# RWKV time mixing: unit-by-unit columns in the mixed tiles of four batches, and another order for the last unit

## The chip, the cores and the metric

One core of a Trainium2 chip runs the kernel. The metric is the device time of one execution in microseconds (us), given as the median of several runs. Beside it stands one profiled execution, whose records give every instruction's start and duration.

## What is computed

x has 16 batches of 2048 tokens of 256 values, in f32. Each token is mixed with the token before it in its batch (zero ahead of the first), once with the weights of R and once with those of V. The result is projected, gated and projected once more. The key projection of the full layer does not reach the output, so the kernel leaves it out.

```python
x_prev[:, 1:, :] = x[:, :-1, :]
xv = x * time_mix_v + x_prev * (1 - time_mix_v)
xr = x * time_mix_r + x_prev * (1 - time_mix_r)
v = xv @ value_weight
r = xr @ receptance_weight
out = (sigmoid(r) * v) @ output_weight
```

## The kernel before

**Tiling.** The tokens are cut into 64 units of 512 tokens, four to a batch; unit g is quarter e = g % 4 of batch b = g // 4. The 256 channels lie on the 128 partitions in two halves, counted by `ko`. So a unit of mixed input is 128 partitions x (2 x 512) bf16 elements, in a shape with the channels on the partitions (x transposed). Time mixing is done up to a factor that the weights `w_bf` absorb: mixed = c * x + x_prev, with one constant c per channel (`c_sb`). Because x_prev is x one column earlier, the second term is the same transposed tile `xt` read with an offset of one token.

**Where the transposed tiles come from.** Batches 0 to 9 are transposed by TensorE (L271) and copied out by ScalarE (L288). Batches 10 to 15 are staged in DRAM in bf16 and come back through two DMA transposes on the SP queue (L253), three batches each. In batches 2 to 9 a column index is (j, c) with token = c * 16 + j (in batches 0 and 1 the same within a unit, token = c * 4 + j); in batches 10 to 15 the columns of `xt` are the tokens in their natural order.

**Pairs of units.** From unit 10 on, two units (1024 tokens) share a mix tile, and the product c * x is made for both units at once, in three pieces of 128x1024: `scale` on VectorE (L353) for half ko = 0 of R, `scale_act` on ScalarE (L631) for half ko = 0 of V (from unit 36 on), and `scale_pool` on GpSimd (L363) for half ko = 1 of both. The sum with x_prev is made unit by unit, on VectorE, by `add` (L375). A mix tile thus has a writer that sees a pair and a writer and a reader that see one unit.

**Batches 10 to 13** (`STAGED_PAIRS`, units 40 to 55) need a special order of columns. Their output is stored per pair of units with eight consecutive tokens to a partition row, so token = q * 8 + h * 4 + i, where q is the output partition (0 to 127), h the unit within the pair, and i runs from 0 to 3. A unit h therefore owns four columns of every eight, in `xt` and, in this kernel, also in the mix tile: `unit_cols` (L319) splits the columns as `(q h i)` and takes one h. Reading a unit out of such a tile means rows of four bf16 elements at a distance of eight. For a pair, `unit_cols` gives the columns back as they are. Batches 0 to 9 and batches 14 and 15 have each unit's columns of the mix tile in rows of 128 or more, without that interleaving.

**One unit's work.** `project` (L383) makes R into the PSUM tile `psum_r`, four matmuls with a moving operand of 128x512 from the mix tile; ScalarE takes the sigmoid into `s_sb` (L651). `project` makes V into `psum_v` in the same way; VectorE multiplies both into `z_sb` (L690). `out_matmuls` (L412) makes the output into `psum_o`, eight matmuls with z as the stationary operand and 256 columns of weight; ScalarE copies it to SBUF (L464), and `store` (L433) sends it out, from the SP queue. Each of `psum_r`, `psum_v` and `psum_o` has one buffer of two banks, and the pool `ps_t` has two of one bank.

**Order.** The program is written out by hand in loop order (the framework's own scheduling is off); within an engine the instructions run in that order. From g = 33 on TensorE's order in iteration g is R of unit g, output of unit g - 2, V of unit g. VectorE's is: scale, sums, z of the unit, sums. The last iterations return to the output of unit g - 1, and outputs of units 60 and 61 go in halves through the `ps_t` pool.

**The last unit** (`last_unit`, L481 on; g = 63) cuts everything finer. R and V of unit 63 are projected in halves of 256 tokens; `receptance(h)` makes a half of R and its sigmoid (L497), `value(h, n)` a half of V and its product z (L503), in pieces of n * 128 columns. `out_part(pool, name, z, b, e, jj, n, copy, queue)` makes n of a unit's four output slots of 128 tokens, copies them with the engine named (`by_act` or `by_dve`, L442) and stores them from the queue named. With n = 2 its stationary operands are z columns with a step of two (`(c j)`); with n = 1 they are 128 columns in a row. z of unit 62 is written in two halves of 256 columns. The four PSUM banks of the half projections are taken up front: `psum_r`, `ps_t`, `psum_v`, `ps_t`.

Two lines carry what the change touches: the layout, and the piece that the last unit's outputs are made of.

```python
return cols.rearrange("p k (q h i) -> p k q h i", h=2, i=UJ)[:, :, :, lo // TU % 2]
order = "p k (j c) -> p k j c" if b < STAGED else "p k (c j) -> p k j c"
```

Of the kernel before, what the change touches and what calls it, by code (L numbers as in the profile page):

```python
# [15 lines left out]
def kernel(  # L16
# [25 lines left out]
    nc = tc.nc  # L42
# [5 lines left out]
    UJ = 4  # L48
    TU = UJ * P
# [5 lines left out]
    H = UJ // 2  # L55
# [41 lines left out]
    ps_t_pool = ctx.enter_context(tc.tile_pool(name="ps_t", bufs=2, space=bass.MemoryType.PSUM))  # L97
    ps_v_pool = ctx.enter_context(tc.tile_pool(name="ps_v", bufs=1, space=bass.MemoryType.PSUM))
    ps_r_pool = ctx.enter_context(tc.tile_pool(name="ps_r", bufs=1, space=bass.MemoryType.PSUM))
    ps_o_pool = ctx.enter_context(tc.tile_pool(name="ps_o", bufs=1, space=bass.MemoryType.PSUM))  # L100
# [12 lines left out]
    xt = {}  # L113
# [199 lines left out]
    def slots(piece, off=0):  # L313

        b, _, lo, hi = piece
        j = lo // P + (lo // TU if b < BYUNIT else 0) + off
        return slice(j, j + (hi - lo) // P)

    def unit_cols(cols, lo, hi):  # L319

        if hi - lo > TU:
            return cols
        assert hi - lo == TU
        return cols.rearrange("p k (q h i) -> p k q h i", h=2, i=UJ)[:, :, :, lo // TU % 2]

    def tokens(piece, off, ko=None):

        b, _, lo, hi = piece
        if b in STAGED_PAIRS:
            pair = lo // (2 * TU) * 2 * TU + off  # L330
            cols = unit_cols(xt[b][:, :, pair : pair + 2 * TU], lo, hi)
            return cols if ko is None else cols[:, ko]
        if b < STAGED:
            cols = xt[b][:, slots(piece, off)]
        else:
            cols = xt[b][:, :, off + lo : off + hi].rearrange("p k (j c) -> p j k c", c=P)
        return cols if ko is None else cols[:, :, ko]

    def mixed(piece, ko=None):
        b, m, lo, hi = piece  # L340
        cols = mix[(b * S + lo) // (2 * TU)][:, m]
        if b in STAGED_PAIRS:
            cols = cols.rearrange("p j k c -> p (j k c)").rearrange("p (k t) -> p k t", k=KO)
            cols = unit_cols(cols, lo, hi)
            return cols if ko is None else cols[:, ko]
        j = lo // P % (2 * UJ)
        cols = cols[:, j : j + (hi - lo) // P]
        return cols if ko is None else cols[:, :, ko]

    def scale(piece, kos=(0, 1)):  # L350
        b, m, _, _ = piece
        for ko in kos:
            nc.vector.tensor_scalar(  # L353
                out=mixed(piece, ko),
                in0=tokens(piece, 0, ko),
                scalar1=c_sb[:, m, ko : ko + 1],
                scalar2=None,
                op0=ALU.mult,
            )

    def scale_pool(piece, after):
        b, m, _, _ = piece
        op = nc.gpsimd.tensor_scalar(  # L363
            out=mixed(piece, 1),
            in0=tokens(piece, 0, 1),
            scalar1=c_sb[:, m, 1:2],
            scalar2=1.0,
            op0=ALU.mult,
            op1=ALU.mult,
        )  # L370
        tc.add_manual_dep(op.ins, after.ins.name, SYNC, reason="one at a time")

    def add(piece):
        b = piece[0]
        return nc.vector.tensor_tensor(  # L375
            out=mixed(piece), in0=mixed(piece), in1=tokens(piece, 1), op=ALU.add
        )

    def project(ps, g, m, lo=0, hi=TU):
        b, e = divmod(g, UB)  # L380
        for mo in range(KO):
            for ko in range(KO):
                nc.tensor.matmul(  # L383
                    out=ps[:, mo, :],
                    lhsT=w_bf[:, m, ko, mo * P : (mo + 1) * P],
                    rhs=mixed((b, m, e * TU + lo, e * TU + hi), ko),
                    start=(ko == 0),
                    stop=(ko == KO - 1),
                )
# [15 lines left out]
    def out_matmuls(ps, z, b, jj, n):  # L405

        cols = z[:, :, jj * P : (jj + n) * P]
        order = "p k (j c) -> p k j c" if b < STAGED else "p k (c j) -> p k j c"
        slot = cols.rearrange(order, j=n)
        for j in range(n):  # L410
            for ko in range(KO):
                nc.tensor.matmul(  # L412
                    out=ps[:, j, :],
                    lhsT=slot[:, ko, j],
                    rhs=wo_bf[:, ko, :],
                    start=(ko == 0),
                    stop=(ko == KO - 1),
                )

    def store(queue, b, lo, hi, after=None):  # L420
        src = o_sb[b, lo // (2 * UJ)]
        j = lo % (2 * UJ)
        src = src[:, j : j + hi - lo, :]
        if b < STAGED:
            dst = out[b].rearrange("(p j) d -> p j d", p=P)[:, lo:hi, :]
        elif b in STAGED_PAIRS:
            h = lo // (2 * UJ)
            dst = out[b, h * 2 * TU : (h + 1) * 2 * TU].rearrange("(p j) d -> p j d", p=P)[:, j : j + hi - lo]
        else:
            n = min(hi - lo, UJ)  # L430
            dst = out[b, lo * P : hi * P].rearrange("(e p j) d -> p e j d", p=P, j=n)
            src = src.rearrange("p (e j) d -> p e j d", j=n)
        op = queue.dma_start(out=dst, in_=src)  # L433
        if after is not None:
            tc.add_manual_dep(op.ins, after.ins.name, SYNC, reason="in turn with the last load")

    def out_part(pool, name, z, b, e, jj, n, copy, queue):
        ps = pool.tile([P, n, D], FP32, name=name)
        out_matmuls(ps, z, b, jj, n)
        lo = e * UJ + jj  # L440
        j = lo % (2 * UJ)
        copy(out=o_sb[b, e // 2][:, j : j + n, :], in_=ps)  # L442
        store(queue, b, lo, lo + n)

    def new_o(b, h):

        n = b * UB // 2 + h - SPARE
        spare = n >= 0 and n % (NO + NX) < NX
        pool, name = (xpool, "x_bf") if spare else (opool, "o_sb")
        o_sb[b, h] = pool.tile([P, 2 * UJ, D], FP32, name=name)  # L450
# [30 lines left out]
    def last_unit(g):  # L481


        b, e = divmod(g, UB)
        new_o(b, e // 2)
        s_sb = zpool.tile([P, KO, TU], BF16, name="s_sb")
        z_sb = zpool.tile([P, KO, TU], BF16, name="z_sb")
        cols = [(h * H * P, (h + 1) * H * P) for h in range(2)]
        spare = [(ps_r_pool, "psum_r"), (ps_t_pool, "ps_t"), (ps_v_pool, "psum_v"), (ps_t_pool, "ps_t")]
        banks = [pool.tile([P, KO, H * P], FP32, name=name) for pool, name in spare]  # L490

        by_act, by_dve = nc.scalar.copy, nc.vector.tensor_copy

        def receptance(h):
            lo, hi = cols[h]
            project(banks[h], g, 0, lo, hi)
            nc.scalar.activation(out=s_sb[:, :, lo:hi], in_=banks[h], func=ACT.Sigmoid)  # L497

        def value(h, n):
            lo, hi = cols[h]  # L500
            project(banks[2 + h], g, 1, lo, hi)
            for c in range(lo, hi, n * P):
                nc.vector.tensor_tensor(  # L503
                    out=z_sb[:, :, c : c + n * P],
                    in0=s_sb[:, :, c : c + n * P],
                    in1=banks[2 + h][:, :, c - lo : c - lo + n * P],
                    op=ALU.mult,
                )

        receptance(0)  # L510
        out_part(ps_o_pool, "psum_o", z_prev, b, e - 1, 0, H, by_dve, nc.sync)
        receptance(1)
        value(0, H)
        out_part(ps_r_pool, "psum_r", z_prev, b, e - 1, H, H, by_act, nc.sync)
        value(1, 1)
        out_part(ps_v_pool, "psum_v", z_sb, b, e, 0, 1, by_act, nc.sync)
        out_part(ps_o_pool, "psum_o", z_sb, b, e, 1, 1, by_act, nc.sync)
        out_part(ps_t_pool, "ps_t", z_sb, b, e, 2, 1, by_act, nc.scalar)
        out_part(ps_t_pool, "ps_t", z_sb, b, e, 3, 1, by_dve, nc.sync)

    def tile_for(b):

# [80 lines left out]
    by_act = {g: [] for g in range(-1, NU)}  # L603
# [35 lines left out]
    for g in range(NU - 1):  # L639
# [47 lines left out]
        z_sb = zpool.tile([P, KO, TU], BF16, name="z_sb")  # L687
# [13 lines left out]
        if g in STAGE_AT:  # L701
            b = STAGE_AT[g]
# [7 lines left out]
        if g == 1:  # L710
            advance(4)
        z_prev2, z_prev = z_prev, z_sb
    last_unit(NU - 1)


# [28 lines left out]
```

## Time and profile before

| | |
|---|---|
| median of 3 runs | 200.34 us (200.04 to 200.56) |
| profiled execution | 200.75 us |
| its span, first to last instruction | 198.9 us |
| TensorE clock granted | 0.997 of full |
| busy share | TensorE 97%, VectorE 92%, ScalarE 89%, GpSimd 44% |
| chain that ended last | TensorE 87%, VectorE 5%, DMA 3% |
| bytes moved by DMA | 58.13 MB, mean 292 GB/s |

All times inside the execution are counted from the start of the span. [...] the distance from one group to the next says more than the duration of one. The chain view does that: it lists the pieces on the way to the last instruction, each with the time that it added.

### The profile page before, as it was taken

To read this page: it belongs to the slowest core of one execution; us is meant where nothing else is said; L and a number is where in the kernel's file an instruction comes from. 1 tells how busy PE (TensorE), PEld (TensorE's weight loads), DVE (VectorE), ACT (ScalarE), POOL (GpSimd) and SP (SyncE) were. 2 spreads that over 40 slices of the span, in tenths; PEclk is the share of its full clock that TensorE was granted. 3 is DMA by queue.
4 is the path that set the end of the run, shared out by engine and by line. 5 is a ranking of instruction groups with operands and counts; after the bars stand their busy time and mean duration, and the time that the engine had idled before them with its cause. 6 is when DMAs were issued, how large, how long until landed. Compare 5 with 4: busy or idle time off the path is not lost.

```text
span 198.9 us, 3759 instructions
## 1 busy us (share of the span) xinstructions
PE 193.8 (97%) x1368; PEld 123.5 (62%) x1368; DVE 183.8 (92%) x287; ACT 177.0 (89%) x197; POOL 86.8 (44%) x117
## 2 busy tenths in 40 slices
PE   8999999999999999999999999999999999999992
PEld 4656676666666666666666566656655666666661
DVE  0899999999999999999999999999999999999972
ACT  3699899999999999999999999998888888899972
POOL 2846442443675634624424474444443344444200
PEclk9999999999999999999999999999999999999998
DMA  5999999999999999999999999999999999999585
GB/s 176 236 184 216 221 278 274 270 256 260 247 384 272 292 315 321 290 226 222 234 276 290 416 293 222 208 273 228 290 340 420 415 412 422 415 417 413 244 319 202
DMA packets 36553, 58.13 MB, mean 292 GB/s; under 512 B 26068, under 2 KB 27448, under 8 KB 32312
## 3 DMA queue, kind: packets, MB, share of 16 engines
q1 hardware_dynamic: 32368, 41.34, 59.7%
q0 software_dynamic: 4016, 16.44, 41.2%
q8 instruction: 10, 0.16, 0.3%
q10 hardware_dynamic: 152, 0.13, 0.2%
q14 instruction: 7, 0.06, 0.1%
HBM read 34.34 MB, written 39.90 MB: 373 GB/s over the span
## 4 chain that ended last, share of the span: by engine, by line
PE 87%; DVE 5%; DMA 3%; SPq 1%; issue 1%; POOL 1%; ACT 1%; DVEq 0%; POOLq 0%
PE psum_v L383 26%; PE psum_r L383 26%; PE psum_o L412 26%; PE ps_t L271 7%; DMA w_f<-in_value_weight_dram 3%; DVE z_sb L690 2%; DVE mix L375 1%; DVE mix L353 1%; SPq L173 1%; PE ps_t L412 1%; ACT s_sb L651 1%; PE ps_t L383 0%; POOL x_bf L161 0%; POOL mix L363 0%; DVE w_bf L587 0%
## 5 line engine op out<-in xcount | busy, mean ns | idle before, releaser
L363 POOL TENSOR_SCALAR mix<-xt_both,c_sb 128x1024 bf16<-128x1024 bf16 (+1 forms) x55 | 61.2, 1113 | 86.8 <-DVE mix L375 74.4
L690 DVE TENSOR_TENSOR z_sb<-s_sb,psum_v 128x1024 bf16<-128x1024 bf16 (+1 forms) x64 | 76.7, 1199 | 3.4 <-PE psum_v L383 2.5
L375 DVE TENSOR_TENSOR mix<-mix,xt_both 128x1024 bf16<-128x1024 bf16 x112 | 76.8, 696 | 1.4
L383 PEld LDWEIGHTS <-w_bf 128*128 128x128 bf16 x516 | 48.7, 97 | 40.2 <-DVE mix L375 0.8
L651 ACT ACTIVATE s_sb<-psum_r 128x1024 bf16<-128x1024 f32 x63 | 65.2, 1035 | 7.5 <-PE psum_r L383 7.2
L383 PE MATMUL psum_v<-mix,w_bf 128*128 128x512 bf16 (+1 forms) x256 | 65.9, 379 | 0.1
L383 PE MATMUL psum_r<-mix,w_bf 128*128 128x512 bf16 (+1 forms) x252 | 64.8, 379 | 0.2 <-DVE mix L375 0.2
L412 PE MATMUL psum_o<-wo_bf,z_sb 128*128 128x256 bf16 x486 | 63.3, 272 | 0.2 <-DVE z_sb L690 0.2
L412 PEld LDWEIGHTS <-z_sb 128*128 128x128 bf16 x512 | 51.7, 103 | 18.6 <-DVE z_sb L503 0.7
L464 ACT COPY o_sb<-psum_o 128x1024 f32<-128x1024 f32 x50 | 51.2, 1024 | 5.1 <-PE psum_o L412 5.1
L288 ACT COPY xt_both<-ps_t 128x1024 bf16<-128x1024 bf16 x32 | 32.8, 1036 | 0.0
L271 PEld LDWEIGHTS <-x_bf 128*128 128x128 bf16 x304 | 19.8, 98 | 8.6 <-DMA x_bf<-in_x_dram 0.7
L271 PE MATMUL ps_t<-ident,x_bf 128*128 128x128 bf16 x304 | 22.7, 219 | 0.3 <-DMA x_bf<-in_x_dram 0.3
L353 DVE TENSOR_SCALAR mix<-xt_both,c_sb 128x1024 bf16<-128x1024 bf16 (+1 forms) x47 | 21.2, 460 | 0.0
L631 ACT ACTIVATE mix<-xt_both,c_sb 128x1024 bf16<-128x1024 bf16 x14 | 16.2, 1161 | 0.0
L375 DVE TENSOR_TENSOR mix<-mix,xt_first 128x1024 bf16<-128x1024 bf16 x15 | 10.6, 714 | 0.1
L464 ACT COPY x_bf<-psum_o 128x1024 f32<-128x1024 f32 x10 | 10.2, 1015 | 0.0
L353 DVE TENSOR_SCALAR mix<-xt_first,c_sb 128x512 bf16<-128x512 bf16 x22 | 6.6, 353 | 0.2
L288 ACT COPY xt_first<-ps_t 128x1024 bf16<-128x1024 bf16 x6 | 6.1, 1024 | 0.0
L161 POOL DMA_DIRECT2D x_bf<-in_x_dram x8 | 5.2, 656 | 0.0
L550 POOL COPY xt_first<-xt_first 128x254 bf16<-128x254 bf16 x5 | 2.0, 395 | 6.8 <-DVE mix L375 6.8
L363 POOL TENSOR_SCALAR mix<-xt_first,c_sb 128x512 bf16<-128x512 bf16 x6 | 4.1, 689 | 1.5 <-DVE mix L375 1.0
(70 smaller groups left out, 54.7 us busy)
## 6 DMA issues: line engine op xcount, KB each, us to landing
out_dram<-o_sb SPq DMA_DIRECT2D x24, 1024.0 KB, 12.8
x_bf<-in_x_dram POOLq DMA_DIRECT2D x8, 1024.0 KB, 16.5
x_natural<-in_x_dram POOLq DMA_DIRECT2D x4, 1024.0 KB, 13.7
out_dram<-x_bf SPq DMA_DIRECT2D x4, 1024.0 KB, 14.5
x_natural<-in_x_dram POOLq DMA_DIRECT2D x4, 512.0 KB, 14.0
x_bf<-in_x_dram POOLq DMA_DIRECT2D x6, 256.0 KB, 6.6
out_dram<-x_bf SPq DMA_DIRECT2D x6, 256.0 KB, 2.2
o_sb<-in_x_dram SPq DMA_DIRECT2D x4, 256.0 KB, 4.1
```

The costliest lines, as they stand in the source:

```text
L161: return nc.gpsimd.dma_start(out=x_bf[b], in_=rows(b), max_dma_last_dim=run)
L271: nc.tensor.transpose(out=ps[:, jj], in_=src[:, jj, ko * P : (ko + 1) * P], identity=idn)
L288: nc.scalar.copy(out=xt[b][:, j0 : j0 + UJ], in_=ps)
L353: nc.vector.tensor_scalar(out=mixed(piece, ko), in0=tokens(piece, 0, ko), scalar1=c_sb[:, m, ko : ko + 1], scalar2=None, op0=ALU.mult,)
L363: op = nc.gpsimd.tensor_scalar(out=mixed(piece, 1), in0=tokens(piece, 0, 1), scalar1=c_sb[:, m, 1:2], scalar2=1.0, op0=ALU.mult, op1=ALU.mult,
L375: return nc.vector.tensor_tensor(out=mixed(piece), in0=mixed(piece), in1=tokens(piece, 1), op=ALU.add)
L383: nc.tensor.matmul(out=ps[:, mo, :], lhsT=w_bf[:, m, ko, mo * P : (mo + 1) * P], rhs=mixed((b, m, e * TU + lo, e * TU + hi), ko), start=(k ...
L412: nc.tensor.matmul(out=ps[:, j, :], lhsT=slot[:, ko, j], rhs=wo_bf[:, ko, :], start=(ko == 0), stop=(ko == KO - 1),)
L464: nc.scalar.copy(out=o[:, j0 : j0 + UJ, :], in_=ps)
L631: nc.scalar.activation(out=mixed(piece, ko), in_=tokens(piece, 0, ko), func=ACT.Copy, scale=c_sb[:, m, ko : ko + 1],)
L651: nc.scalar.activation(out=s_sb, in_=ps_r, func=ACT.Sigmoid)
L690: nc.vector.tensor_tensor(out=z_sb[:, :, c : c + n], in0=s_sb[:, :, c : c + n], in1=ps_v[:, :, c : c + n], op=ALU.mult,)
```

## The change

In batches 10 to 13 the mix tile's columns are put as `(h q i)`: unit 0's 512 columns come first, then unit 1's. `xt` keeps `(q h i)`. `unit_cols` gets the order as an argument, and now also splits the columns of a pair, so that the products of a pair are read in one order and written in the other. The columns that `project` reads, and that `add` reads and writes in the mix tile, are then in one row per `ko`; `add` still reads x_prev out of `xt` in rows of four.

In the last unit the order of the pieces changes: both halves of R, then the first half of the output of unit 62 (copied by ScalarE, not VectorE), both halves of V, the second half of output 62, and output 63 in three pieces (slots 0 and 1 together, slot 2, slot 3) where there were four. The pair of slots goes through `psum_v` and ScalarE, the two single ones through `ps_t` and VectorE; the last store is issued from ScalarE's queue.

```diff
-    def unit_cols(cols, lo, hi):
-
+    def unit_cols(cols, order, lo, hi):
+
+        cols = cols.rearrange(f"p k ({order}) -> p k q h i", h=2, i=UJ)
         if hi - lo > TU:
             return cols
         assert hi - lo == TU
-        return cols.rearrange("p k (q h i) -> p k q h i", h=2, i=UJ)[:, :, :, lo // TU % 2]
+        return cols[:, :, :, lo // TU % 2]
...
             pair = lo // (2 * TU) * 2 * TU + off
-            cols = unit_cols(xt[b][:, :, pair : pair + 2 * TU], lo, hi)
+            cols = unit_cols(xt[b][:, :, pair : pair + 2 * TU], "q h i", lo, hi)
...
             cols = cols.rearrange("p j k c -> p (j k c)").rearrange("p (k t) -> p k t", k=KO)
-            cols = unit_cols(cols, lo, hi)
+            cols = unit_cols(cols, "h q i", lo, hi)
...
         receptance(0)
-        out_part(ps_o_pool, "psum_o", z_prev, b, e - 1, 0, H, by_dve, nc.sync)
         receptance(1)
+        out_part(ps_o_pool, "psum_o", z_prev, b, e - 1, 0, H, by_act, nc.sync)
         value(0, H)
+        value(1, 1)
         out_part(ps_r_pool, "psum_r", z_prev, b, e - 1, H, H, by_act, nc.sync)
-        value(1, 1)
-        out_part(ps_v_pool, "psum_v", z_sb, b, e, 0, 1, by_act, nc.sync)
-        out_part(ps_o_pool, "psum_o", z_sb, b, e, 1, 1, by_act, nc.sync)
-        out_part(ps_t_pool, "ps_t", z_sb, b, e, 2, 1, by_act, nc.scalar)
-        out_part(ps_t_pool, "ps_t", z_sb, b, e, 3, 1, by_dve, nc.sync)
+        out_part(ps_v_pool, "psum_v", z_sb, b, e, 0, H, by_act, nc.sync)
+        out_part(ps_t_pool, "ps_t", z_sb, b, e, 2, 1, by_dve, nc.sync)
+        out_part(ps_t_pool, "ps_t", z_sb, b, e, 3, 1, by_dve, nc.scalar)
```

## Prediction

> **What bounds the kernel now.** I read the page's busy shares and its chain first:
>
> ```profile
> PE 193.8 (97%) x1368; PEld 123.5 (62%) x1368; DVE 183.8 (92%) x287; ACT 177.0 (89%) x197; POOL 86.8 (44%) x117
> PE 87%; DVE 5%; DMA 3%; SPq 1%; issue 1%; POOL 1%; ACT 1%; DVEq 0%; POOLq 0%
> ```
>
> TensorE is the bound, and VectorE stands close behind. The two parts of the change lie in different stretches, so I then took the chain in order of time around units 40 and 56, where batches 10 to 13 begin and end:
>
> ```profile
> 127.42 0.87 PE psum_o L412 x8
> 128.29 0.86 PE psum_v L383 x4
> 129.15 0.90 PE psum_r L383 x4
> 130.05 0.87 PE psum_o L412 x8
> 130.93 0.90 PE psum_v L383 x4
> ...
> 173.71 0.86 PE psum_v L383 x4
> 174.58 0.86 PE psum_r L383 x4
> ```
>
> From unit 40 (129.15) on, four matmuls of a projection take 0.90 us in place of 0.86; outputs stay at 0.87. The step ends at 171.98, with unit 56. So reading rows of four columns costs TensorE something. Busy time by stretch, 16 units and then 4:
>
> ```profile
> 129.15:171.98 42.83, 42.83 (x258) 26.14 (x256) 41.53 (x57) 38.45 (x41) 17.95 (x16) 1.00 1.08 354
> 171.98:182.38 10.40, 10.40 (x65) 6.63 (x64) 10.27 (x14) 9.47 (x11) 4.49 (x4) 1.00 1.01 415
> ```
>
> Columns: length, then PE, PEld, DVE, ACT, POOL busy. A unit takes 42.83/16 = 2.677 us in the first and 10.40/4 = 2.600 in the second. In the second VectorE is busy 99%: once TensorE is faster, it is the next bound. Its slack is in the timeline of one pair:
>
> ```profile
> 131.00 0.48 DVE L353 TENSOR_SCALAR mix<-xt_both,c_sb 128x1024 bf16<-128x1024 bf16 x1
> 131.40 0.68 DVE L375 TENSOR_TENSOR mix<-mix,xt_both 128x1024 bf16<-128x1024 bf16 x1
> ...
> 132.18 1.12 POOL L363 TENSOR_SCALAR mix<-xt_both,c_sb 128x1024 bf16<-128x1024 bf16 x1 [1.64 <-DVE mix L375]
> ...
> 133.13 1.31 DVE L375 TENSOR_TENSOR mix<-mix,xt_both 128x1024 bf16<-128x1024 bf16 x2
> ...
> 134.61 1.22 DVE L690 TENSOR_TENSOR z_sb<-s_sb,psum_v 128x1024 bf16<-128x1024 bf16 x1 [0.17 <-PE psum_v L383]
> ```
>
> The pair before starts its z at 129.26; 134.61 less 0.17 of waiting is 134.44, and starts overlap the operation ahead by 0.08, so VectorE needs about 134.36 - 129.26 = 5.10 us a pair. TensorE needs 5.35 now and 5.20 at the faster rate: 0.10 of slack would remain.
>
> For the last unit I read the timeline and the DMA's rate by stretch:
>
> ```profile
> 191.22 0.10 PEld L412 LDWEIGHTS <-z_sb 128*128 128x128 bf16 x1
> 191.75 0.23 PEld L412 LDWEIGHTS <-z_sb 128*128 128x128 bf16 x3 [0.43 <-DVE z_sb L690]
> ...
> 193.97 0.33 PEld L412 LDWEIGHTS <-z_sb 128*128 128x128 bf16 x4 [0.26 <-DVE z_sb L503]
> ```
>
> and, with the rate in GB/s as the last column:
>
> ```profile
> 195.05:195.75 0.70, 0.26 (x2) 0.00 (x0) 0.41 (x1) 0.34 (x2) 0.00 (x0) 1.00 0.97 372
> 195.75:197.45 1.70, 0.00 (x0) 0.00 (x0) 0.02 (x1) 0.00 (x0) 0.00 (x0) 1.00 0.90 309
> ```
>
> Two readings. First, output 62's first half needs only the first half of z 62, yet its second weight load waits until 191.75, when the second half ends (191.01 + 0.68): these loads take every second column, and the wait that the program attaches covers more than it reads. Output 63's loads, 128 columns in a row, go at 193.97, while z's last pieces are still to come. Second, the last 768 KB (half of output 62, four quarters of 63) leave without a gap from 195.05 to 197.4: a half, rows of 2 KB, takes 0.70 us, each quarter, rows of 1 KB, 0.40. The end follows that stream.
>
> [...] The scale takes 0.48 us for 1024 elements and 0.35 for 512 (L353 in the groups): 0.25 ns an element, [...] Adds on rows of four take 0.68 us here, as do those on rows of 128; no run here shows the scale so. [...]
>
> **Part A, the layout.** *TensorE:* 16 units x 8 matmuls on one row of 512 in place of 128 rows of four. 16 x (2.677 - 2.600) = **-1.22 us**, all on the chain; bounds -1.3 and 0 (if the row is still read as before). *Add*, 32 of them: two operands become plain rows; 0.69 us mean on plain rows, so nothing. *Scale on VectorE*, 8 of 0.48 us, now writing rows of four: from 0.48 [...] to 0.74 at half rate [...]. Up to 0.58 the 0.10 of slack hides it. *Scale on ScalarE*, 8 of 1.16: 0.86 ns an element (0.72 us for 512), and ScalarE is idle for 42.83 - 38.45 us, 0.55 a pair; nothing. *Scale on GpSimd*, 16 of 1.12, idle 1.3 to 1.6 before each: for V (126.98 to 128.10) the add that needs it starts at 128.56, so it may grow to 1.55. Bounds 1.12 (taken) and 1.98, if its 0.84 ns an element (0.69 us for 512) doubles. *DMA:* units finish 1.2 us earlier. The transpose of batches 13 to 15 lands about 149.3 (issued 134.41, 14.9 to landing), and its first reader is GpSimd in iteration 49, from 153.2: 0.7 earlier still leaves over 3 us. Stores come earlier by up to 1.2 us, when the DMA is full; it has caught up by 185.5, where its rate falls to 82 GB/s, so the extra 512 KB is gone before the tail. Nothing.
>
> **Part B, the last unit.** In before's clock. TensorE starts R at 190.89, and each of the half groups follows by 0.44. *Removed:* the stall of 0.32 in front of output 62 (second R covers it: R1 ends its stream at 191.76, z 62 at 191.75). R1 needs the bank that output 61's copy frees at 191.24, and starts 191.32: 0.08 of cover. *Then:* output 62a 191.76, V0 192.19, V1 192.63, output 62b 193.07 (was 192.96: V1 is now ahead of it). ScalarE takes sigmoid 0 (191.61), sigmoid 1 (192.10), copy 62a (192.60, to 193.19; by VectorE it ended 192.98), copy 62b (193.70, to 194.29; was 194.19). So 62b's store goes 0.10 later, 194.31, and its data start 195.15. VectorE: z of V0 192.90 to 193.59, pieces of V1 193.50 and 193.84, ending 194.26.
>
> *Added wait:* slots 0 and 1 of output 63 are one group now, with every second column. By the reading above its second weight load waits for the last piece of z: 194.31, not 193.64. Behind it in TensorE's order stand its other matmuls and slots 2 and 3; ScalarE's copy and the 256 KB store wait for it. It ends 194.82, copied 194.85 to 195.44, issued on SP 195.47, data from 196.31 (0.84 from issue to data, as 194.21 to 195.05 now). Slot 2 (TensorE 194.65 to 195.04, VectorE 195.07 to 195.50) is issued on SP behind it at 195.89 (spacing 0.42); slot 3, copied 195.41 to 195.84, goes from ScalarE's queue at 195.86, where nothing else is queued. VectorE gives up one copy of 0.69 and takes on one more quarter (0.43); ScalarE changes three quarters of 0.37 for two halves of 0.59; both end ahead of these stores. Five stores in place of six, same bytes: 196.31 + 0.70 + 2 x 0.40 = 197.8 against 197.4: **+0.40 us**. Without that wait the half's data follow 62b's at once: 195.15 + 2 x 0.70 + 0.80 = 197.35, so -0.05. I take +0.40 and keep -0.10 and +0.50 for the range.
>
> Sum: -1.22 + 0.40 = -0.82. The execution behind the sum took 200.75 (198.9 of span and 1.85 around it), 0.41 above the median; it would come to 199.93. The same step from the median 200.34 gives **199.5 us**.
>
> **Rivals.** *The half does not wait* (its one evidence is output 62's load): -1.22 - 0.05, 199.1. [...] 5.10 + 0.26 = 5.36 us a pair against 5.35 now, so part A gives nothing, B's 0.40 remains: 200.8, slower. It decides from a scale of 0.68: 5.30 a pair, and the 8 x 0.05 saved equals the 0.40 lost. [...] For it: nothing shows such a write, slack is 0.10. Against: adds at the same rows pay nothing. *GpSimd falls to half rate on those writes:* 1.98, 0.86 more, less 0.46 to the add and 0.10 of slack, 0.30 x 8 = 2.4: 200.34 + 2.4 - 0.82 = 201.9. For it: no run here shows such a write. Against: at 0.84 ns an element it asks a third of what VectorE's 0.25 asks of the memory. *TensorE still reads at 0.90:* B alone, 200.7. Against: 0.86 wherever columns lie in rows of 128.
>
> **Numbers.** A measurement of this kernel tells 0.3% (0.6 us) from no change, so faster means under 199.74. Main case 0.55; no wait 0.23; VectorE 0.09; GpSimd 0.06; TensorE as before 0.04; the rest between. The main case is 0.2 from the bound, and I give it 0.46 faster, 0.09 same; no wait is faster; a partial loss at VectorE or TensorE as before are the rest of same: faster 0.70, same 0.17, slower 0.13. Range 198.9 (B's and A's best ends with some spread) to 200.8 [...].
>
> **What would show it.** Right: projections at 0.86 throughout the chain; L353 at 0.48, L363 at 1.12, L631 at 1.16 in units 40 to 55; no wait on VectorE beyond 0.2; output 62 without its 0.43; the first half of output 63 starting one load, then waiting some 0.65 us for the last z. Wrong: any of the scales longer, or weight loads of L412 for slots 0 and 1 all together.

## The result, and the profile after

The changed kernel takes **214.88 us** (median of 4 runs, 214.71 to 214.93); the kernel before takes 200.22 (200.04 to 200.56) beside it. The ratio is **1.073** (95% interval 1.071 to 1.075): 14.7 us slower, where 0.8 us faster was forecast. Six of the lines named below stand one line further down than before: `scale` L354, `scale_pool` L364, `add` L376, `project` L384, `out_matmuls` L413, z of the last unit L504. The scale on ScalarE (L631), the sigmoid (L651) and z (L690) keep theirs.

The busy shares, TensorE's busy time in 40 equal slices (a digit is the share in tenths) and the chain, from the page of the changed kernel:

```profile
span 213.0 us, 3756 instructions
PE 193.1 (91%) x1368; PEld 122.7 (58%) x1368; DVE 183.8 (86%) x287; ACT 176.6 (83%) x196; POOL 86.5 (41%) x117
PE   8999999999999999999999996697669766999991
PE 82%; DVE 12%; issue 1%; ACT 1%; POOL 1%; DVEq 0%; ACTq 0%; POOLq 0%
```

No engine does more work than before. TensorE is even busy 0.7 us less (193.1 against 193.8) and VectorE exactly as long (183.8). What is new is idle time, and the third line says where: the slices with sixes and sevens lie in the stretch of units 40 to 55. So the added time is a wait, not work. Which wait, the groups say (busy, mean ns of one, then idle time before them and what ended it):

```profile
L384 PE MATMUL psum_r<-mix,w_bf 128*128 128x512 bf16 (+1 forms) x252 | 65.6, 378 | 14.2 <-DVE mix L376 14.2
...
L384 PE MATMUL psum_v<-mix,w_bf 128*128 128x512 bf16 (+1 forms) x256 | 65.3, 377 | 0.1
```

Before the matmuls of R TensorE stands idle for 14.2 us, and a sum on VectorE ends all of it; before those of V, 0.1. The waits of the stretch from 90 to 205 us (total, number, longest):

```profile
ACT s_sb L651 <- PE psum_r L384: 21.6, 16, 2.4
PEld L384 <- DVE mix L376: 18.1, 8, 2.3
...
PE psum_r L384 <- DVE mix L376: 14.2, 8, 1.8
```

Eight waits of 1.77 us: one in each of the eight pairs of batches 10 to 13. The timeline of the first pair (start, duration, engine, line, operands; idle time before it in brackets):

```profile
127.57 1.30 DVE L376 TENSOR_TENSOR mix<-mix,xt_both 128x1024 bf16<-128x1024 bf16 x2
...
127.76 1.03 PE L384 MATMUL psum_v<-mix,w_bf 128*128 128x512 bf16 x4
...
128.62 0.38 PE L384 MATMUL psum_r<-mix,w_bf 128*128 128x512 bf16 x1
128.90 1.22 DVE L690 TENSOR_TENSOR z_sb<-s_sb,psum_v 128x1024 bf16<-128x1024 bf16 x1
...
130.03 0.68 DVE L376 TENSOR_TENSOR mix<-mix,xt_both 128x1024 bf16<-128x1024 bf16 x1
130.64 0.49 DVE L354 TENSOR_SCALAR mix<-xt_both,c_sb 128x1024 bf16<-128x1024 bf16 x1
130.77 0.33 PEld L384 LDWEIGHTS <-w_bf 128*128 128x128 bf16 x3 [2.26 <-DVE mix L376]
130.77 0.82 PE L384 MATMUL psum_r<-mix,w_bf 128*128 128x512 bf16 x3 [1.77 <-DVE mix L376]
...
133.44 1.22 DVE L690 TENSOR_TENSOR z_sb<-s_sb,psum_v 128x1024 bf16<-128x1024 bf16 x1 [1.72 <-PE psum_v L384]
```

One matmul of R of unit 40 goes at 128.62, right behind V of unit 39. The other three wait until 130.77, 0.06 after the sum that starts at 130.03 ends. That sum belongs to R of unit **41**, the neighbour in the pair. Unit 40's own sums, of R and of V, are the two that start at 127.57; the one for R was done by about 128.25, before R's first matmul at 128.62. Unit 41's sum can't come sooner: VectorE takes z of unit 39 ahead of it, and z starts only when V of unit 39 is done (128.90). So TensorE waits for VectorE, and then VectorE waits 1.72 us for V of unit 40, once in every pair. From the second pair on, a pair takes 7.14 us (z to z over two units) in place of 5.35.

The layout shows why the two are tied. With `(k h q i)` the odd unit's sum writes columns 512 to 1023 and 1536 to 2047, and between them lie 1024 to 1535, the even unit's half ko = 1, which the second matmul reads. The trace has that matmul's weight load released by the odd unit's sum (the `PEld` line at 130.77, 2.26 us), although no column is common to both. In the kernel before, with rows of four at a distance of eight on both sides, neither TensorE nor its weight loads wait for a sum in this stretch (the waits from 90 to 205 us list none).

**Theories.** T1: this attached wait makes the whole loss: 8 x 1.77 us of standing still, and 0.17 a pair more (7.14 - 5.20 - 1.77), which it puts down to starting again. T2, its rival: the new rows themselves (a row of 512 read, writes cut into rows of four) cost time, and the wait only shows it. T3: the last unit's new order does it.

### The profile page after: what moved, and what is told of

It is laid out like the page before. It is cut to its first block, busy times and chain, and to the rows that moved or that the text cites. A ratio compares the mean times of both kernels' runs of the same rounds, so it can differ in the third digit from the quotient of the medians.

```text
span 213.0 us, 3756 instructions
## 1 busy us (share of the span) xinstructions
PE 193.1 (91%) x1368; PEld 122.7 (58%) x1368; DVE 183.8 (86%) x287; ACT 176.6 (83%) x196; POOL 86.5 (41%) x117
## 4 chain that ended last, share of the span: by engine, by line
PE 82%; DVE 12%; issue 1%; ACT 1%; POOL 1%; DVEq 0%; ACTq 0%; POOLq 0%
PE psum_v L384 24%; PE psum_r L384 24%; PE psum_o L413 23%; PE ps_t L271 7%; DVE z_sb L690 6%; DVE mix L376 4%; PE ps_t L203 1%; DVE mix L354 1%; PE ps_t L413 1%; PE psum_r L398 1%; PE psum_r L299 1%; ACT xt_first L281 1%; ACT x_bf L465 0%; PE ps_t L384 0%; POOL x_bf L161 0%
## 5 line engine op out<-in xcount | busy, mean ns | idle before, releaser
L364 POOL TENSOR_SCALAR mix<-xt_both,c_sb 128x1024 bf16<-128x1024 bf16 (+1 forms) x55 | 61.0, 1109 | 101.3 <-DVE mix L376 74.6
L690 DVE TENSOR_TENSOR z_sb<-s_sb,psum_v 128x1024 bf16<-128x1024 bf16 (+1 forms) x64 | 76.8, 1201 | 17.3 <-PE psum_v L384 16.3
L651 ACT ACTIVATE s_sb<-psum_r 128x1024 bf16<-128x1024 f32 x63 | 65.2, 1035 | 21.8 <-PE psum_r L384 21.6
L384 PEld LDWEIGHTS <-w_bf 128*128 128x128 bf16 x516 | 48.2, 98 | 55.1 <-DVE mix L376 18.5
L384 PE MATMUL psum_r<-mix,w_bf 128*128 128x512 bf16 (+1 forms) x252 | 65.6, 378 | 14.2 <-DVE mix L376 14.2
L376 DVE TENSOR_TENSOR mix<-mix,xt_both 128x1024 bf16<-128x1024 bf16 x112 | 76.5, 694 | 1.4
L384 PE MATMUL psum_v<-mix,w_bf 128*128 128x512 bf16 (+1 forms) x256 | 65.3, 377 | 0.1
L413 PE MATMUL psum_o<-wo_bf,z_sb 128*128 128x256 bf16 x484 | 62.8, 273 | 0.0
L413 PEld LDWEIGHTS <-z_sb 128*128 128x128 bf16 x512 | 51.9, 103 | 17.5 <-DVE z_sb L504 0.3
L465 ACT COPY o_sb<-psum_o 128x1024 f32<-128x1024 f32 x50 | 51.2, 1024 | 5.0 <-PE psum_o L413 5.0
L354 DVE TENSOR_SCALAR mix<-xt_both,c_sb 128x1024 bf16<-128x1024 bf16 (+1 forms) x47 | 21.3, 461 | 0.0
L631 ACT ACTIVATE mix<-xt_both,c_sb 128x1024 bf16<-128x1024 bf16 x14 | 16.3, 1162 | 0.0
L376 DVE TENSOR_TENSOR mix<-mix,xt_first 128x1024 bf16<-128x1024 bf16 x15 | 10.6, 714 | 0.1
L354 DVE TENSOR_SCALAR mix<-xt_first,c_sb 128x512 bf16<-128x512 bf16 x22 | 6.5, 348 | 0.3 <-ACT xt_first L281 0.2
L364 POOL TENSOR_SCALAR mix<-xt_first,c_sb 128x512 bf16<-128x512 bf16 x6 | 4.1, 685 | 0.7 <-DVE mix L376 0.2
```

The source lines that it names most:

```text
L354: nc.vector.tensor_scalar(out=mixed(piece, ko), in0=tokens(piece, 0, ko), scalar1=c_sb[:, m, ko : ko + 1], scalar2=None, op0=ALU.mult,)
L364: op = nc.gpsimd.tensor_scalar(out=mixed(piece, 1), in0=tokens(piece, 0, 1), scalar1=c_sb[:, m, 1:2], scalar2=1.0, op0=ALU.mult, op1=ALU.mult,
L376: return nc.vector.tensor_tensor(out=mixed(piece), in0=mixed(piece), in1=tokens(piece, 1), op=ALU.add)
L384: nc.tensor.matmul(out=ps[:, mo, :], lhsT=w_bf[:, m, ko, mo * P : (mo + 1) * P], rhs=mixed((b, m, e * TU + lo, e * TU + hi), ko), start=(k ...
L413: nc.tensor.matmul(out=ps[:, j, :], lhsT=slot[:, ko, j], rhs=wo_bf[:, ko, :], start=(ko == 0), stop=(ko == KO - 1),)
L465: nc.scalar.copy(out=o[:, j0 : j0 + UJ, :], in_=ps)
```

## The experiments

### The two halves of the change alone

`a_alone` keeps the layout and puts the old last unit back; `b_alone` is the kernel before with the new last unit. Their diffs are the two parts of the change's diff.

> The change's layout of batches 10 to 13 with the old last unit. T1 (the layout gives the even unit of each pair a wait on its odd neighbour's sum, which it doesn't read: 8 pairs x 1.77 us): 214.9 us, the whole loss, with the wait of R's matmuls on the add at 14 us. T2 (the new rows themselves cost TensorE or VectorE time): also about 214.9, so this run doesn't part T1 from T2. T3 (the last unit brings the loss): under 201. The prediction's own step A: 199.1.

Measured: 214.84 us, ratio 1.071 (1.0687 to 1.0734), with the wait of R's matmuls on the sum at 14.2 us as in the change.

> The old layout with the new last unit. T1 and T2: within 0.2 us of before, 200.2, because the tail in the changed kernel took 6.57 us from the start of its first R to the last data, 6.55 before. The prediction's added wait for output 63's first half: +0.40, 200.6. T3: 214 or more.

Measured: 200.82 us, ratio 1.002 (1.0005 to 1.0034); the kernel before took 200.59 beside it. The loss is the layout's. T3 falls. The last unit by itself costs 0.1 to 0.7 us by the interval; in the traces the time from its first R to the end of the span is 8.01 us before, 8.13 here and 8.15 in the change, so 0.1.

### The same rows, but each unit in one block

`row512`: the change with the unit outside ko, so that a unit's two rows lie side by side.

```diff
-            cols = cols.rearrange("p j k c -> p (j k c)").rearrange("p (k t) -> p k t", k=KO)
-            cols = unit_cols(cols, "h q i", lo, hi)
+            cols = cols.rearrange("p j k c -> p (j k c)")
+            cols = cols.rearrange("p (h k q i) -> p k q h i", h=2, k=KO, i=UJ)
+            if hi - lo == TU:
+                cols = cols[:, :, :, lo // TU % 2]
             return cols if ko is None else cols[:, ko]
```

> The change with one thing altered: in the mix tile of batches 10 to 13 each unit is one block of 1024 columns (h k q i in place of k h q i), so that both ko of a unit lie together. TensorE still reads a row of 512, and the scales and sums still write and read the same rows of four and of 512; but a unit's sum no longer reaches across its neighbour's columns. T1: the wait is gone, projections at 0.86 per four, about 199.0 (200.2 - 1.2). T2: rows unchanged, so the loss stays, about 214. In between if both hold.

Measured: **199.38 us, ratio 0.9943 (0.9929 to 0.9957)**, 1.2 us faster than before. The wait is gone, and the projections go at 0.86 all through, four matmuls of 379 ns mean each, so their records overlap (the chain view around unit 40):

```profile
126.35 0.86 PE psum_r L386 x4
127.21 0.87 PE psum_o L415 x8
128.09 0.86 PE psum_v L386 x4
128.95 0.86 PE psum_r L386 x4
```

The eight pairs from z of unit 38 to z of unit 54 (length, then PE, PEld, DVE, ACT, POOL busy), in the change and in `row512`:

```profile
126.44:183.45 57.01, 42.84 (x257) 25.59 (x256) 41.97 (x57) 38.16 (x40) 19.02 (x17) 1.00 0.98 317
```

```profile
126.62:168.20 41.58, 41.58 (x257) 26.28 (x256) 41.46 (x58) 38.32 (x41) 18.00 (x16) 1.00 1.09 339
```

57.01 us against 41.58 (and 42.66 before): 15.4 us between two kernels that differ in one thing: the even unit's second row and the odd unit's first have changed places. `row512` has the same row of 512 for TensorE and the same rows of four written by the scales. T2 falls: those rows cost nothing. Between before and the change the stretch grows by 57.01 - 42.66 = 14.35, which is the loss but for 0.3: 15.4 lost on the wait, 1.1 gained on the reads.

### Rows of 128 with both ko inside

`rows128`: before, with the mix tile of these batches laid out as in the others. The mix tile is written in rows of 128; the scale then has to gather rows of four from `xt`.

```diff
-            cols = unit_cols(xt[b][:, :, pair : pair + 2 * TU], lo, hi)
+            cols = xt[b][:, :, pair : pair + 2 * TU]
+            cols = cols.rearrange("p k (j q h i) -> p k h j q i", j=UJ, h=2, i=UJ)
+            if hi - lo == TU:
+                cols = cols[:, :, lo // TU % 2]
...
+            if hi - lo > TU:
+                return cols[:, :, ko].rearrange("p (h j) (q i) -> p h j q i", h=2, i=UJ)
...
```

> Before with the mix tile of batches 10 to 13 laid out unit by unit in rows of 128 with both ko inside each, the layout that the other batches have; the last unit is the old one. T1: no wait on a neighbour, projections at 0.86 per four, about 199.0. T2 (only a row of 512 or its cut-up writes cost): 199.0 too, and row512 stays at 214. If the scale that reads rows of four and writes rows of 128 costs VectorE more than 0.58 us, above 199.5.

Measured: 200.44 us, ratio 0.9998 (0.9986 to 1.001). No wait on a neighbour, and projections at 0.86 as T1 has it, but for V of the odd unit, which takes 0.95 in the chain (at 129.80); still nothing gained. The profiled execution (201.96 us) lost 1.5 us before its first z, outside this stretch. The timeline of VectorE in a pair, with V of the odd unit:

```profile
128.47 1.21 DVE L688 TENSOR_TENSOR z_sb<-s_sb,psum_v 128x1024 bf16<-128x1024 bf16 x1
...
129.73 1.02 PE L381 MATMUL psum_v<-mix,w_bf 128*128 128x512 bf16 x4
130.86 1.22 DVE L688 TENSOR_TENSOR z_sb<-s_sb,psum_v 128x1024 bf16<-128x1024 bf16 x1
...
132.00 0.73 DVE L373 TENSOR_TENSOR mix<-mix,xt_both 128x1024 bf16<-128x1024 bf16 x1
132.65 0.61 DVE L351 TENSOR_SCALAR mix<-xt_both,c_sb 128x1024 bf16<-128x1024 bf16 x1
133.18 0.68 DVE L373 TENSOR_TENSOR mix<-mix,xt_both 128x1024 bf16<-128x1024 bf16 x1
133.78 1.21 DVE L688 TENSOR_TENSOR z_sb<-s_sb,psum_v 128x1024 bf16<-128x1024 bf16 x1
```

A pair takes 5.31 us, in two parts. From z of the even unit to z of the odd one 2.39: z ends at 129.68, V of the odd unit, which has to wait for it since `psum_v` has one buffer, starts 0.05 later and ends at 130.75, and z of the odd unit follows 0.11 after that. Then 2.92 of VectorE's own: z, sum, scale, sum, where `row512` has 2.74 (129.06 to 131.80). The scale takes 0.61 in place of 0.48, and the sum ahead of it 0.73 in place of 0.69. This comes near the prediction's rival in which VectorE becomes the bound, but by a scale that reads rows of four (0.61) and not by one that writes them (0.49 in `row512`), and in another layout than the change's.

### The wait put off: the odd sums later in the program

`late_r`: the change, with each odd unit's R sum written after the even unit's projection of R. If a wait is attached only to what stands earlier in the program, this takes it away; VectorE's own order, tiles and addresses stay.

```diff
...
             project(ps_r, g, 0)
+        for p in late[0][g]:
+            add(p)
         s_sb = zpool.tile([P, KO, TU], BF16, name="s_sb")
```

> The change, with the sum of the odd unit's R recorded only after the even unit's projection of R; VectorE's order and all tiles as in the change. The wait of R's second matmul on that sum is gone, the same wait of V's second matmul on the odd unit's V sum is left. T1: the stall moves to V and is smaller there, a pair 6.4 us in place of 7.14 and 5.20, so 199.4 + 8 x 1.2 = 209. If R's wait alone made the loss: 199.4.

Measured: 209.03 us, ratio 1.0431 (1.0418 to 1.0444). The waits of the same stretch:

```profile
PEld L384 <- DVE mix L376: 11.4, 8, 1.4
PE psum_v L384 <- DVE mix L376: 8.3, 8, 1.0
```

R waits no more, and V does, on the odd unit's V sum, which the R wait had hidden. Eight pairs take 51.12 us (126.44 to 177.56), 6.39 each: 8 x 1.19 over the 5.20 of `row512`, for 8.3 us of standing still and the starts after it.

`late_rv` moves the odd unit's V sum behind the projection of V as well.

> late_r with the odd unit's V sum recorded after the even unit's projection of V too. TensorE waits for no neighbour's sum any more, but that sum now stands behind the last matmul of V on VectorE, so VectorE's row is cut: by T1 a pair of about 5.55, 202.3. T2 (the new rows cost by themselves): 209 or more, with no wait to name.

Measured: 202.46 us, ratio 1.0122 (1.0093 to 1.0151), 5.56 a pair.

```profile
PEld L384 <- DVE z_sb L704: 3.6, 8, 0.5
DVE mix L376 <- PE psum_v L384: 2.2, 8, 0.3
PE psum_v L384 <- DVE z_sb L704: 1.5, 8, 0.2
```

TensorE waits for no neighbour's sum. Now VectorE's late sum waits for V's matmuls (second line), again, by the layout, a pair of instructions that share no column, and z goes later behind it. With one wait of two taken away 5.9 us of the 15.5 over `row512` go, with both 12.4: the loss follows the waits, with the rows unchanged throughout.

### What ties the sum to the neighbour

`split_sum`: the change, with an odd unit's sum made by two instructions, one for each ko.

```diff
-        b = piece[0]
+        b, _, lo, hi = piece
+        if b in STAGED_PAIRS and hi - lo == TU and lo // TU % 2:
+            for ko in range(KO):
+                last = nc.vector.tensor_tensor(
+                    out=mixed(piece, ko), in0=mixed(piece, ko), in1=tokens(piece, 1, ko), op=ALU.add
+                )
+            return last
```

> The change with one thing altered: the sum of each odd unit of batches 10 to 13 is made by two instructions of 512 elements, one for each ko, in place of one of 1024 over two rows. Tiles, layout, order and last unit stay. T1 in the form that one instruction's rows are taken with the gap between them (columns 512 to 2047 for the odd unit, which has the even unit's second row inside): no instruction reaches across any more, so the wait is gone; VectorE pays for two more instructions a pair, about 0.08 each, 5.10 + 0.16 = 5.26 a pair: 199.4 + 8 x 0.06 = 199.9. If the wait is on the tile or on rows that touch, not on the gap: 214.9 as before.

Measured: 200.42 us, ratio 1.0 (0.9985 to 1.0016). The wait on the sum is gone, in the change's own layout, but TensorE's saving is eaten by VectorE. Its timeline in one pair, with V of the odd unit:

```profile
131.78 1.22 DVE L696 TENSOR_TENSOR z_sb<-s_sb,psum_v 128x1024 bf16<-128x1024 bf16 x1
...
133.05 1.02 PE L390 MATMUL psum_v<-mix,w_bf 128*128 128x512 bf16 x4
134.18 1.22 DVE L696 TENSOR_TENSOR z_sb<-s_sb,psum_v 128x1024 bf16<-128x1024 bf16 x1
...
135.31 0.80 DVE L378 TENSOR_TENSOR mix<-mix,xt_both 128x512 bf16<-128x512 bf16 x2
...
136.04 0.49 DVE L354 TENSOR_SCALAR mix<-xt_both,c_sb 128x1024 bf16<-128x1024 bf16 x1
136.44 0.75 DVE L378 TENSOR_TENSOR mix<-mix,xt_both 128x512 bf16<-128x512 bf16 x2
137.11 1.21 DVE L696 TENSOR_TENSOR z_sb<-s_sb,psum_v 128x1024 bf16<-128x1024 bf16 x1
```

The same two parts: 2.40 from z through `psum_v` to z, and 2.93 of VectorE's own, 0.19 more than in `row512`. So each extra instruction costs 0.1 (0.08 was the author's estimate; in the trace of before, z of unit 62 in two halves takes 1.28 us and z in one piece 1.22), and the pair is 5.33 in place of 5.26. Without the extra it would be 2.40 + 2.74 = 5.14, not the prediction's 5.10.

`gap_64`: the change, with 64 unused columns between the two ko rows.

```diff
...
-            cols = cols.rearrange("p j k c -> p (j k c)").rearrange("p (k t) -> p k t", k=KO)
+            cols = flat.rearrange("p (k t) -> p k t", k=KO)[:, :, : 2 * TU]
...
-            mix[b] = mixpool.tile([P, 2, 2 * UJ, KO, P], BF16, name="mix")
+            mix[b] = mixpool.tile([P, 2, KO * (2 * TU + GAP)], BF16, name="mix")
```

> The change with 64 unused columns between the two ko rows of every mix tile of batches 10 to 13, so that the odd unit's first row no longer touches the even unit's second. T1 with the gap between an instruction's rows taken as written: the wait stays, a pair 7.14, 214.9. If only rows that touch are merged: the wait is gone, 199.4.

Measured: 215.16 us, ratio 1.0726 (1.071 to 1.0742), a pair 7.15, and R's matmuls wait 14.2 us on the sum as in the change. That the rows touch isn't the reason. In this layout the weight loads waited as if what lies between the two rows of an odd unit's sum were written by it (18.1 us in the change and in `gap_64`): with the neighbour's columns elsewhere (`row512`) or one row written at a time (`split_sum`), no such wait is left. This is no full rule: with rows of four at a distance of eight, in the kernel before, the neighbour's columns also lie in between, and no wait shows. The last unit has a second exception: z's last pieces are two rows of 128 at a distance of 512, output 63's first loads read between them, and those loads did not wait (shown further down). Where the line runs was not settled.

### The last unit on the better layout

`row512_old` is `row512` with the old last unit; `row512_c` has the second half of output 62 ahead of the second half of V.

```diff
+        out_part(ps_r_pool, "psum_r", z_prev, b, e - 1, H, H, by_act, nc.sync)
         value(1, 1)
-        out_part(ps_r_pool, "psum_r", z_prev, b, e - 1, H, H, by_act, nc.sync)
```

> row512 (each unit of batches 10 to 13 one block of 1024 columns) with the old last unit: whether the new last unit gains or costs, apart from the layout. If it is worth nothing (6.57 against 6.55 us from the start of R to the last data): 199.4 as row512, or 0.1 less. If its added wait cost 0.40 as predicted: 199.0. If the new last unit gains: above 199.5.

> row512 with the second half of output 62 ahead of the second half of V (order R, R, half of 62, V, half of 62, V, 63 in three pieces). If the stream of stores that begins with that half sets the end, it now begins some 0.4 us earlier and the end comes 0.2 to 0.4 earlier: 199.0 to 199.2. If the chain through V, z and output 63 sets it: 199.4 or a little later, since V's second half goes 0.44 later.

Measured: 199.35 us, ratio 0.9952 (0.9937 to 0.9966), and 199.39, ratio 0.9949 (0.9935 to 0.9963). Three orders of the last unit, one time. From the first R to the end of the span they take 8.14 (`row512`), 8.08 (`row512_old`) and 8.11 us (`row512_c`). In `row512_c` the copy of 62's second half starts 0.50 earlier (191.78 against 192.28, each counted from an R 0.07 apart, so 0.43), and the end doesn't follow. That the stores beginning with that half alone set the end is refuted; what else does was not followed up, since at most 0.1 us hangs on it. `row512` stays the fastest layout, and each of its last units beats both kernels.

## Why the prediction was wrong

**The step that failed** is in part A: "*Add*, 32 of them: two operands become plain rows; 0.69 us mean on plain rows, so nothing." The price of the instruction was right (0.68 in the change). But the step priced instructions only. It took over the waits of the old layout without asking, for each instruction that changes shape, who is tied to it now. The sum of -1.22, "all on the chain", held the same silent premise, and none of the rivals was a new wait in this stretch. The mechanism stood in the text: "the wait that the program attaches covers more than it reads". It was read off output 62 and applied to output 63 alone, not to the sums of the odd units, which got the form of output 62's writer: z's second half is two rows of 256 (columns 256 to 511 and 768 to 1023), and the load that waited reads between them. Applied to the sums, in an estimate made from the trace of the change, it gives R of the even unit behind z of the unit before and the sum (1.13 + 0.68 us from z's start to the sum's end, 130.71): some 1.8 us of wait in each of 8 pairs, 14 us, and the sign of the forecast turns. The runs put the loss at 15.5 us between the change and `row512`. The range, 198.9 to 200.8, left such a wait out altogether.

**TensorE's reads, -1.22:** right. From z of unit 38 to z of unit 56 the kernel before takes 48.01 us and `row512` 46.78: -1.23 (the prediction's own product, 16 x (2.677 - 2.600), is 1.23 too). Rows of four cost 0.04 us in four matmuls (0.90 against 0.86), one row of 512 nothing (0.86 in `row512`). What makes the rows of four dearer isn't shown.

**The scales:** right. Writing rows of four leaves L354 at 0.49, L364 at 1.12, L631 at 1.16 (means in the stretch from 128.60 to 185.95). Both rivals on these writes, a slower scale on VectorE (0.74, so 200.8) and on GpSimd (1.98, so 201.9), are refuted. Both times were the author's estimates, from 0.25 and 0.84 ns an element in the trace of before and a doubling that no run shows.

**VectorE's slack, 0.10 a pair:** mis-sized; it is 0.06. The prediction summed VectorE's own work to 5.10. The loop also passes through TensorE: z of the even unit frees `psum_v`, V of the odd unit fills it, z of the odd unit follows, 2.40 for that and 2.74 for the rest, 5.14 against TensorE's 5.20. In the change, where VectorE idles, this cost nothing; it is why `rows128` (0.18 more) and `split_sum` (0.19 more) came to 5.31 and 5.33 and gained next to nothing.

**Part B, +0.40:** the order came out as worked out, to 0.02 us: the first half of output 62 0.88 after R's start (0.87 predicted), its second half 2.19 (2.18), that half copied at 3.41 (3.40). The added wait did not come. z's last pieces and the weight loads of output 63 in the changed kernel:

```profile
207.47 0.74 DVE L504 TENSOR_TENSOR z_sb<-s_sb,ps_t 128x256 bf16<-128x256 bf16 x2
207.61 0.78 PEld L413 LDWEIGHTS <-z_sb 128*128 128x128 bf16 x8 [0.26 <-DVE z_sb L504]
```

All eight in a row, those of slots 0 and 1 and behind them those of slots 2 and 3, started by the end of z's first half, while the last pieces run until 208.21: the sign named for the rival "the half does not wait", with -0.05 to its name. The loads of slots 0 and 1 take every second column here, as output 62's do, so a step of two does not by itself attach a wait. By the traces the last unit's part is +0.1, by `row512` against `row512_old` zero within their intervals, by `b_alone`'s interval 0.1 to 0.7: at most a small cost, and no gain shown.

## What to carry to other kernels

When a layout changes, list for every instruction not only what it costs but which waits the program attaches to it, and do so for writers that skip over a neighbour's columns: here TensorE was held back by a sum whose two rows enclosed the data that it read, and the standing still alone came to 14 us, with no engine busier than before. The repair was free with the block of one producer made contiguous (unit outside ko, 1.2 us faster than before), while splitting the instruction cost VectorE what it won (200.42 us, ratio 1.0). Idle time beside unchanged busy sums (VectorE 183.8 us in both kernels) was a wait here; take the releaser's name from the groups, then ask whose data that releaser wrote.

## What the runs showed that was not expected

- The side on which the scale meets rows of four made a difference. Reading a row and writing rows of four takes VectorE 0.49 us for 1024 elements (`row512`); gathering rows of four and writing rows of 128 takes 0.61 (`rows128`), though the sum gathers such rows at 0.68 without loss. In the kernel's code `xt` begins at column PAD - 1 = 15 of its tile, and the scale reads with off = 0, the sum with off = 1. So it is the scale that takes x_prev, and the sum that adds x (mixed = c * x_prev + x, the other way round than told at the start). It also means that the scale's rows of four begin at an odd column, the sum's at an even one. No run tried the scale's gather from an even column, so that this is the cause isn't shown.
- A wait can hide a second one of its own kind: R's 14.2 us hid 8.3 us at V, which only `late_r` brought out. Taking away the wait that the profile names gave back 5.9 us of 15.5.
